# Attention queries turned once in the projection, and the row of maxima moved within SBUF

## The chip, the core and the metric

The kernel runs on one core of one Trainium2 chip. The metric is the device time of one execution in microseconds. Engines are called by the profile's names: PE (matmuls), DVE (vector work), ACT (activations and copies), POOL (vector work of the GpSimd engine), SP (it issues DMAs).

## What is computed

One layer of a transformer over 2048 latent tokens with 256 context tokens, width 1024, all in float32. A modulated RMSNorm feeds one projection whose columns are keys, values, queries, two halves of a gated MLP and two gates. Attention has eight query heads on two key/value heads, 64 wide; queries and keys are normalised and rotated (rope). A merge and a squared-ReLU MLP follow. What the change touches:

```python
q_x = apply_rope(rmsnorm(q_heads(q_x), q_norm_g[l]), cos, sin) * q_scale
k_all = jnp.concatenate([k_c, k_x], axis=2)
v_all = jnp.concatenate([v_c, v_x], axis=2)
attn_x = merge_heads(attend_blocked(q_x, k_all, v_all))   # softmax over 2304 keys
```

## The kernel before

A float32 operand is split into a high part (the cast to the fast matmul type) and a remainder, and products are sums of several matmuls. The span has three stretches: the projection with the gated MLP's mixing and the first part of the gates (to about 757 us), attention (to about 1436 us), and merge and MLP.

**In the projection**, `queries_work` (L770) treats one block of 512 tokens at a time, four blocks in all: it loads the raw queries, normalises them and applies rope on DVE in two halves c of 256 columns, tokens on the partitions. Each half is stored by SP to the DRAM tensor `q_d`, shaped [512 tokens, 512 columns] per block (L788). Such helpers are generators; the main loop of matmuls advances them step by step, and a scheduler then fixes the order on each engine by priority and dependences.

**Attention** runs over 16 units, one per block of 512 queries and pair of heads. A unit works through 18 tiles j of 128 keys in three groups of six (`GROUP`). Scores are made turned, with keys on the partitions and queries along the row, in two accumulating matmuls per head: `first` (L2034) multiplies the stacked high and low keys by `qa`, a tile in which the high part of a head's turned queries stands twice, in partitions 0 to 63 and 64 to 127; `second` (L2053) multiplies by `qb`, whose row 0 holds the negated maximum of each query, rows 1 to 63 zeros and rows 64 to 127 the turned remainder. The keys' counterpart of row 0 is a row of ones, from `lead`. So the maximum is subtracted inside the matmul, and ACT takes the exponential at once (L2057). `values` (L2067) follow after each group, sums of exponentials are added up on POOL and DVE (L2083, L2080).

What a unit needs is prepared by the units ahead of it. `load` brings a unit's queries from `q_d` in one transfer (L1948) and clears a tile `pb` on POOL (L1956). `cast` writes the high part twice into `pa` on ACT (L1959), and `remainder` writes the low part into `pb` on DVE (L1962). `queries` turns `pa` with eight transposes on PE (the helper at L189, `ident` is the identity) and two copies on ACT (L1974) into `qa`. `maxima` multiplies queries by keys a second time, unturned (L1999), and reduces on DVE (L2010, L2005 for the context). `reference` reduces these to one number per query (L2016) and writes it negated into column 0 of `pb` (L2017). `low_queries` turns `pb` with eight more transposes and two copies into `qb`.

`attend` (L1124) writes the order out by hand: in unit i, the unit after the next (`far`) is loaded in group 0 behind tile 2, its `cast` and `remainder` come in group 0, its `queries` in group 1 behind tile 8; the next unit's (`nxt`) `reference` ends group 1, its `low_queries` come in group 2 behind tile 17. PE and DVE keep the written order inside attention (`order`); the other engines are ordered by the scheduler. For units 0 and 1 the same steps are placed in `tail` (L1758), at the end of the projection. In units 1 to 4 DVE also works on the modulation weights (`mod`, L364, L368) in the middle of groups. The score banks of PSUM come from a rotating set of eight.

Of the kernel before, what the change touches and what calls it, by code (L numbers as in the profile page):

```python
# [10 lines left out]
F32 = mybir.dt.float32  # L11
F32R = mybir.dt.float32r
# [39 lines left out]
def f32(ap):  # L52
    return ap.bitcast(F32)
# [17 lines left out]
class Kern:  # L71
# [119 lines left out]
    def constants(self):  # L191
# [8 lines left out]
        nc.vector.memset(self.ones, 1.0)  # L200
        self.lead = cp.tile([P, 1], F32, name="lead")
        nc.vector.memset(self.lead, 0.0)
        nc.vector.memset(self.lead[0:1], 1.0)
        self.G1 = cp.tile([P, KC, 2], F32, name="G1")
        self.S1 = cp.tile([P, KC, 2], F32, name="S1")
        self.G2 = cp.tile([P, KC], F32, name="G2")
# [8 lines left out]
        def spill(n, shape):  # L215
            return [dp.tile(shape, F32, tag=f"{n}{b}", name=f"{n}_d{b}") for b in range(NB)]

        self.q_d = spill("q", [TB, NH * HD])
        self.gm_d = spill("gm", [512, TB])
        self.at_d = spill("at", [512, TB])  # L220
        self.ta_d = spill("ta", [D, TB])
# [548 lines left out]
    def queries_work(self, b):  # L770
        nc = self.nc
        q = [self.m4([TT, 4, HD]) for _ in range(2)]
        flat = [x.rearrange("p t h d -> p t (h d)") for x in q]
        src = self.pr_d[0][b]
        nc.sync.dma_start(flat[0][:, :, :P], self.rows(src[0], slice(2 * P, 3 * P)))
        nc.sync.dma_start(flat[0][:, :, P:], self.rows(src[1], slice(0, P)))
        nc.sync.dma_start(flat[1], self.rows(src[1], slice(P, 3 * P)))
        yield
        yield
        rbs = self.heads_rstd(q, 1.0 / HD)  # L780
        yield
        tabs = self.rope_tables("q", b)
        for c, (raw, rb) in enumerate(zip(q, rbs)):
            nc.vector.tensor_tensor(out=raw, in0=raw, in1=rb, op=ALU.mult)
            yield
            qo = self.m4([TT, 4, HD])
            self.rope(tabs, raw, qo, self.m4([TT, 4, HD]), 4)
            nc.sync.dma_start(  # L788
                self.rows(self.q_d[b], slice(c * 256, (c + 1) * 256)),
                qo.rearrange("p t h d -> p t (h d)"),  # L790
            )
            yield

    def raw_values(self, b, j, c):
        x = self.m4([TT, 4, HD])
# [328 lines left out]
    def attend(self, units, late, mod):  # L1124
        self.psum({"b": 8})
        begin = self.here()
        pend = []
        for i, u in enumerate(units):
            at = lambda n: units[n] if 0 <= n < len(units) else None
            nxt, far, old, older = at(i + 1), at(i + 2), at(i - 1), at(i - 2)  # L1130
            for gi, g in enumerate(range(0, NKT, GROUP)):
                group = range(g, g + GROUP)
                step = nxt if gi < 2 else far
                for j in group:
                    u.first(j)
                    u.second(j)
                    if j % GROUP == 2 and far:
                        if gi == 0:
                            far.load()
                        elif gi == 1:  # L1140
                            far.queries()
                    if not nxt:
                        next(late, None)
                    elif i and j % GROUP == 4:
                        next(mod, None)
                if gi == 2 and nxt:
                    nxt.low_queries()
                if step:
                    step.maxima(3)
                for f in pend:  # L1150
                    f()
                if gi == 0 and far:
                    far.cast()
                if gi == 2 and old:
                    old.sums()
                if step:
                    step.maxima(3)
                if gi == 0:
                    if older:
                        older.inverse()  # L1160
                    if far:
                        far.remainder()
                if gi == 1:
                    if nxt:
                        nxt.reference()
                    if old:
                        old.join()
                pend = [lambda u=u, j=j: u.values(j) for j in group]
            pend.append(u.leave)
        for _ in mod:  # L1170
            pass
# [558 lines left out]
    def build(self):  # L1730
# [27 lines left out]
        def tail(g, p):  # L1758
            u, v = units[0], units[1]
            n = KC - 2  # L1760
            if (g, p) == (n + 1, 0):
# [1 line left out]
                key_load(0)  # L1763
                u.cast()
                u.remainder()
            elif (g, p) == (n, 1):
                u.queries()
            elif (g, p) == (n + 1, 1):
                low_load(0)
            elif (g, p) == (n, 5):  # L1770
# [1 line left out]
            elif g >= n and p not in (0, 1):  # L1772
                if (g, p) == (n + 1, 5):
# [1 line left out]
                    v.cast()  # L1775
                    v.remainder()
                    value_load((0, 1))
                if (g, p) == (n, 6):
                    v.queries()
# [6 lines left out]
                if (g, p) == (n + 1, 3):  # L1786
                    u.maxima(len(u.todo))
                    u.reference()
                    u.low_queries()
                    v.maxima(6)  # L1790

        self.project(tail)
# [142 lines left out]
class Unit:  # L1935
# [8 lines left out]

    def load(self):
        k, nc = self.k, self.nc
        self.qt = k.t2([TT, 2, HD])
        nc.sync.dma_start(  # L1948
            self.qt.rearrange("p t h d -> p t (h d)"),
            k.q_d[self.b].rearrange("(t p) c -> p t c", p=P)[  # L1950
                :, :, self.p * P : (self.p + 1) * P
            ],
        )
        self.pa = k.t4([TT, 2, 2, HD], F32R)
        self.pb = k.t4([TT, 2, P])
        nc.gpsimd.memset(self.pb[:, :, :, :HD], 0.0)  # L1956

    def cast(self):
        self.nc.scalar.copy(self.pa, self.qt.unsqueeze(3).broadcast_to([P, TT, 2, 2, HD]))  # L1959

    def remainder(self):
        self.nc.vector.tensor_tensor(  # L1962
            out=self.pb[:, :, :, HD:], in0=self.qt, in1=f32(self.pa[:, :, :, 0, :]),
            op=ALU.subtract,
        )

    def turned(self, src):
        k = self.k
        out = []
        for h in range(2):  # L1970
            ps = k.bank([TB])
            k.transposes(ps, [src(t, h) for t in range(TT)])
            q = k.h2([TB], F32R)
            self.nc.scalar.copy(q, ps)  # L1974
            out.append(q)
        return out

    def queries(self):
        self.qa = self.turned(
            lambda t, h: f32(self.pa[:, t, h]).rearrange("p a d -> p (a d)")  # L1980
        )
        self.mx = self.k.small([TT, 2, NB + 1])

    def maxima(self, n):
        k, nc = self.k, self.nc
# [26 lines left out]
                    )  # L2012

    def reference(self):
        nm = self.k.small([TT, 2])
        self.nc.vector.tensor_reduce(out=nm, in_=self.mx, axis=AX.X, op=ALU.max)  # L2016
# [158 lines left out]
```

## Time and profile before

| | |
|---|---|
| time, median of 3 runs | 3094.04 us (3090.9 to 3099.88) |
| profiled execution, time | 3104.55 us |
| its span | 3102.5 us |
| its mean granted clock on PE | 0.983 |
| PE busy | 2994.0 us, 97% |
| DVE busy | 2074.6 us, 67% |
| ACT busy | 1459.5 us, 47% |
| POOL busy | 689.0 us, 22% |

Times in the profile are microseconds from the start of the span of one profiled execution. A row of the timeline gives start, duration, engine, line of the kernel, operation, what is written and read, shapes and count, and in brackets the idle time ahead of it with what ended it. Matmuls overlap, so the time that PE spends on one is read from the start of it to the start of the next.

### The profile page before, as it was taken

What the parts mean: (1) busy time and instruction counts of PE and PEld (TensorE: products, weight loads), DVE (VectorE), ACT (ScalarE), POOL (GpSimd) and SP (SyncE); (2) the same over time, 40 slices, a digit from 0 to 9 for tenths busy, and PEclk for the clock granted to TensorE, in tenths of its full rate; (3) what the DMA queues carried; (4) which work ended last, traced back from release to release, by engine and by line L of the source; (5) the groups of instructions that cost most, each with busy time, mean ns of one, the idle gap of its engine ahead of it and who ended that gap; (6) DMA issues with size and microseconds to landing.
All of it is one profiled execution on the core that took longest, in us unless ns stands there. A gap on an engine that the chain in (4) does not pass through costs nothing.

```text
span 3102.5 us, 38027 instructions
## 1 busy us (share of the span) xinstructions
PE 2994.0 (97%) x13501; PEld 2262.9 (73%) x13501; DVE 2074.6 (67%) x2990; ACT 1459.5 (47%) x2352; POOL 689.0 (22%) x506
## 2 busy tenths in 40 slices
PE   6999999979999999999989999999999999999999
PEld 4877788766555555556867878887878888878887
DVE  4767578875887667777654478775676666654555
ACT  5645765654555454554222155443454344444432
POOL 0000000001988888885134300000000000000000
PEclk9999999999999999999999999999999999999999
DMA  8676666644110000005865448887776544438554
GB/s 296 202 259 212 226 197 198 205 145 129 35 35 28 14 15 8 11 15 185 265 203 164 137 156 316 310 301 278 256 234 220 191 153 153 154 139 285 204 200 153
DMA packets 386478, 534.32 MB, mean 172 GB/s; under 512 B 32928, under 2 KB 204112, under 8 KB 386288
## 3 DMA queue, kind: packets, MB, share of 16 engines
q1 hardware_dynamic: 376512, 515.89, 49.7%
q10 hardware_dynamic: 9776, 16.01, 1.4%
q8 instruction: 106, 1.74, 0.2%
q14 instruction: 84, 0.69, 0.1%
HBM read 367.69 MB, written 164.10 MB: 171 GB/s over the span
## 4 chain that ended last, share of the span: by engine, by line
PE 83%; DMA 6%; DVE 5%; ACT 2%; issue 2%; POOL 1%; SPq 0%; ACTq 0%; DVEq 0%; POOLq 0%
PE b L1502 14%; PE b L1503 14%; PE b L1504 14%; PE b L2067 8%; PE b L2034 5%; PE b L2053 4%; PE b L183 3%; PE b L185 3%; PE b L184 3%; PE a L1502 3%; PE b L1999 3%; PE a L1503 3%; PE a L1504 3%; PE b L189 2%; DMA bw<-in_w_br_gm 1%
## 5 line engine op out<-in xcount | busy, mean ns | idle before, releaser
L2010 DVE TENSOR_REDUCE ts<-b 128x1 f32<-128x512 f32 x512 | 314.7, 681 | 141.6 <-PE b L1999 141.5
L2083 POOL TENSOR_TENSOR ac<-ac,p 128x512 f32<-128x512 f32 x216 | 301.5, 1428 | 67.7 <-ACT p L2057 67.0
L1608 DVE TENSOR_TENSOR b<-b,b 128x1024 fp32r<-128x1024 f32 x168 | 198.6, 1221 | 145.0 <-ACT b L1607 144.6
L1607 ACT CAST b<-b 128x1024 fp32r<-128x1024 f32 x168 | 168.7, 1051 | 240.0 <-PE b L1503 222.0
L2057 ACT ACTIVATE p<-b 128x512 f32<-128x512 f32 x384 | 199.8, 616 | 166.5 <-PE b L2053 156.6
L1502 PE MATMUL b<-b,b 128*128 128x512 f32 x672 | 263.9, 393 | 8.6 <-ACT b L1607 7.9
L1503 PE MATMUL b<-b,b 128*128 128x512 f32 x672 | 263.1, 391 | 2.4 <-DVE b L1608 2.4
L1504 PE MATMUL b<-b,b 128*128 128x512 f32 x672 | 262.6, 391 | 0.0
L2083 POOL TENSOR_TENSOR ac<-ac,t 128x512 f32<-128x512 f32 x152 | 217.6, 1457 | 0.0
L2034 PE MATMUL b<-h,h 128*128 128x512 f32 x576 | 200.9, 419 | 0.9 <-DVE ts L2010 0.4
L2053 PE MATMUL b<-h,h 128*128 128x512 f32 x576 | 180.3, 394 | 0.0
L2067 PE MATMUL b<-p,h 128*64 128x512 f32 x768 | 175.3, 598 | 0.0
L1503 PE MATMUL b<-hb,b 128*128 128x512 f32 x448 | 174.6, 390 | 0.0
L1956 POOL MEMSET t<- 128x512 f32 x16 | 8.4, 525 | 701.9 <-DMA tb_d<-t 679.8
L1502 PE MATMUL b<-hb,b 128*128 128x512 f32 x416 | 162.0, 389 | 0.0
L1504 PE MATMUL b<-hb,b 128*128 128x512 f32 x416 | 161.7, 389 | 0.0
L1512 DVE TENSOR_TENSOR f<-f,b 128x512 f32<-128x512 f32 x160 | 109.2, 682 | 77.7 <-issue 46.1
L1502 PEld LDWEIGHTS b<-b,b 128*128 128x128 f32 x672 | 126.9, 189 | 36.6 <-ACT b L1607 9.2
L2034 PEld LDWEIGHTS b<-h,h 128*128 128x128 f32 x576 | 106.7, 190 | 58.4 <-DVE ts L2010 19.4
L1503 PEld LDWEIGHTS b<-b,b 128*128 128x128 f32 x672 | 126.8, 189 | 30.0 <-DVE b L1608 3.7
L1504 PEld LDWEIGHTS b<-b,b 128*128 128x128 f32 x672 | 126.8, 189 | 26.5
L1502 PE MATMUL a<-f,h 128*128 128x384 f32 (+1 forms) x320 | 118.7, 376 | 12.8 <-ACT f L647 6.3
(409 smaller groups left out, 7435.0 us busy)
## 6 DMA issues: line engine op xcount, KB each, us to landing
ao_d<-f SPq DMA_DIRECT2D x224, 256.0 KB
f<-in_w_ff SPq DMA_DIRECT2D x48, 1024.0 KB
b<-ao_d SPq DMA_DIRECT2D x84, 512.0 KB
b<-w2o_d SPq DMA_DIRECT2D x84, 512.0 KB
w2o_d<-f SPq DMA_DIRECT2D x112, 256.0 KB
f<-in_w_in SPq DMA_DIRECT2D x44, 512.0 KB
f<-x_d SPq DMA_DIRECT2D x64, 256.0 KB
hb<-ao_d SPq DMA_DIRECT2D x56, 256.0 KB
```

The lines of the kernel that those rows point to most:

```text
L1502: mm(ps, wh, hh, start=start and k == 0, stop=False, skip_group_check=True)
L1503: mm(ps, wh, hl, start=False, stop=False, skip_group_check=True)
L1504: mm(ps, wl, hh, start=False, stop=k == len(w) - 1, skip_group_check=True)
L1512: nc.vector.tensor_tensor(out=out, in0=in0, in1=in1, op=op)
L1607: nc.scalar.copy(h, f32(l))
L1608: nc.vector.tensor_tensor(out=l, in0=f32(l), in1=f32(h), op=ALU.subtract)
L2010: nc.vector.tensor_reduce(out=self.mx[:, t, h, c : c + 1], in_=ps[h], axis=AX.X, op=ALU.max)
L2034: self.nc.tensor.matmul(self.pts[j][h], k.KA[c][self.kv][:, ks], self.qa[h], start=True, stop=False, skip_group_check=True,)
L2053: self.nc.tensor.matmul(s, k.KB[c][self.kv][:, ks], self.qb[h], start=False, stop=True, skip_group_check=True,)
L2057: self.nc.scalar.activation(pt[h], s, AF.Exp)
L2067: nc.tensor.matmul(self.o[h * HD : (h + 1) * HD, :], k.V[c][:, i, self.kv * HD : (self.kv + 1) * HD], pt[h], start=j == 0, stop=j == NKT - 1,)
L2083: nc.gpsimd.tensor_tensor(out=self.acc[e][:, h], in0=old[:, h], in1=pt[h], op=ALU.add)
```

## The change

In `queries_work` each rotated half is now turned on PE, four transposes for each pair of heads, copied from PSUM by ACT and stored through ACT's DMA queue, so that `q_d` holds, for each block and pair, the queries turned: 128 rows (two heads of 64) by 512 tokens. A unit's `load` fetches each head's 64 rows twice, into both halves of a tile's partitions, in four transfers on SP. `cast` (two copies on ACT, now in group 1) gives `qa` directly, `remainder` (two subtractions on DVE, now at the end of group 2) gives `qb` directly. `pa`, `pb` and `low_queries` go. The remainder also stands in rows 0 to 63 of `qb` now; rows 1 to 63 meet zeros of `lead`. Row 0 is overwritten with the maxima by the new `leading`, placed behind tile 14: one transpose of 128x8 to 8x128 on PE, a copy on ACT, and eight transfers of 512 bytes within SBUF on SP, each to a stretch of 128 queries in row 0. The sign of the maxima moves into `lead`, which is -1 instead of 1, so L2017 goes.

```diff
-        nc.vector.memset(self.lead[0:1], 1.0)
+        nc.vector.memset(self.lead[0:1], -1.0)
...
-        self.q_d = spill("q", [TB, NH * HD])
+        self.q_d = [
+            [dp.tile([P, TB], F32, tag=f"q{b}_{p}", name=f"q_d{b}_{p}") for p in range(NH // 2)]
+            for b in range(NB)
+        ]
...
             self.rope(tabs, raw, qo, self.m4([TT, 4, HD]), 4)
-            nc.sync.dma_start(
-                self.rows(self.q_d[b], slice(c * 256, (c + 1) * 256)),
-                qo.rearrange("p t h d -> p t (h d)"),
-            )
-            yield
+            yield
+            for f in range(2):
+                ps = self.bank([TB])
+                self.transposes(
+                    ps,
+                    [
+                        qo[:, t, 2 * f : 2 * f + 2].rearrange("p h d -> p (h d)")
+                        for t in range(TT)
+                    ],
+                )
+                ot = self.t2([TB])
+                nc.scalar.copy(ot, ps)
+                nc.scalar.dma_start(self.q_d[b][2 * c + f], ot)
...
-                    if j % GROUP == 2 and far:
-                        if gi == 0:
-                            far.load()
-                        elif gi == 1:
-                            far.queries()
+                    if j % GROUP == 2 and far and gi == 0:
+                        far.load()
+                    if j % GROUP == 2 and nxt and gi == 2:
+                        nxt.leading()
...
-                if gi == 2 and nxt:
-                    nxt.low_queries()
...
-                if gi == 0 and far:
+                if gi == 1 and far:
                     far.cast()
...
-                    if far:
-                        far.remainder()
+                if gi == 2 and far:
+                    far.remainder()
...
     def load(self):
         k, nc = self.k, self.nc
-        self.qt = k.t2([TT, 2, HD])
-        nc.sync.dma_start(
-            self.qt.rearrange("p t h d -> p t (h d)"),
-            k.q_d[self.b].rearrange("(t p) c -> p t c", p=P)[
-                :, :, self.p * P : (self.p + 1) * P
-            ],
-        )
-        self.pa = k.t4([TT, 2, 2, HD], F32R)
-        self.pb = k.t4([TT, 2, P])
-        nc.gpsimd.memset(self.pb[:, :, :, :HD], 0.0)
+        self.raw = [k.t2([TB]) for _ in range(2)]
+        for h, raw in enumerate(self.raw):
+            src = k.q_d[self.b][self.p][h * HD : (h + 1) * HD]
+            for i in range(2):
+                nc.sync.dma_start(raw[i * HD : (i + 1) * HD], src)
 
     def cast(self):
-        self.nc.scalar.copy(self.pa, self.qt.unsqueeze(3).broadcast_to([P, TT, 2, 2, HD]))
+        self.qa = [self.k.h2([TB], F32R) for _ in range(2)]
+        for q, raw in zip(self.qa, self.raw):
+            self.nc.scalar.copy(q, raw)
+        self.mx = self.k.small([TT, 2, NB + 1])
 
     def remainder(self):
-        self.nc.vector.tensor_tensor(
-            out=self.pb[:, :, :, HD:], in0=self.qt, in1=f32(self.pa[:, :, :, 0, :]),
-            op=ALU.subtract,
-        )
+        self.qb = [self.k.h2([TB], F32R) for _ in range(2)]
+        for q, hi, raw in zip(self.qb, self.qa, self.raw):
+            self.nc.vector.tensor_tensor(out=q, in0=raw, in1=f32(hi), op=ALU.subtract)
...
     def reference(self):
-        nm = self.k.small([TT, 2])
-        self.nc.vector.tensor_reduce(out=nm, in_=self.mx, axis=AX.X, op=ALU.max)
-        self.nc.vector.tensor_scalar(
-            out=self.pb[:, :, :, 0:1], in0=nm.unsqueeze(3), scalar1=-1.0, scalar2=None,
-            op0=ALU.mult,
-        )
-
-    def low_queries(self):
-        self.qb = self.turned(lambda t, h: self.pb[:, t, h, :])
+        k, nc = self.k, self.nc
+        self.nm = k.small([2, TT])
+        nc.vector.tensor_reduce(
+            out=self.nm.rearrange("p h t -> p t h"), in_=self.mx, axis=AX.X, op=ALU.max
+        )
+
+    def leading(self):
+        k, nc = self.k, self.nc
+        n = 2 * TT
+        ps = k.bank([P])
+        nc.tensor.transpose(ps[:n], self.nm.rearrange("p h t -> p (h t)"), k.ident)
+        row = k.t2([P])
+        nc.scalar.copy(row[:n], ps[:n])
+        for h in range(2):
+            for t in range(TT):
+                nc.sync.dma_start(
+                    f32(self.qb[h])[0:1, t * P : (t + 1) * P],
+                    row[h * TT + t : h * TT + t + 1],
+                )
```

In `tail` the calls of `queries` go, and `low_queries` becomes `leading`.

More of the change, by code (lines that the diff above doesn't have):

```diff
@@ L1765, in tail @@
                 u.remainder()
-            elif (g, p) == (n, 1):
-                u.queries()
             elif (g, p) == (n + 1, 1):
@@ L1777, in tail @@
                     value_load((0, 1))
-                if (g, p) == (n, 6):
-                    v.queries()
                 if (g, p) == (n + 1, 6):
@@ L1788, in tail @@
                     u.reference()
-                    u.low_queries()
+                    u.leading()
                     v.maxima(6)
@@ L1946, in load @@
         k, nc = self.k, self.nc
-        self.qt = k.t2([TT, 2, HD])
-        nc.sync.dma_start(
-            self.qt.rearrange("p t h d -> p t (h d)"),
-            k.q_d[self.b].rearrange("(t p) c -> p t c", p=P)[
-                :, :, self.p * P : (self.p + 1) * P
-            ],
-        )
-        self.pa = k.t4([TT, 2, 2, HD], F32R)
-        self.pb = k.t4([TT, 2, P])
-        nc.gpsimd.memset(self.pb[:, :, :, :HD], 0.0)
+        self.raw = [k.t2([TB]) for _ in range(2)]
[3 more added lines that the diff above has]
+                nc.sync.dma_start(raw[i * HD : (i + 1) * HD], src)
     def cast(self):
-        self.nc.scalar.copy(self.pa, self.qt.unsqueeze(3).broadcast_to([P, TT, 2, 2, HD]))
+        self.qa = [self.k.h2([TB], F32R) for _ in range(2)]
+        for q, raw in zip(self.qa, self.raw):
+            self.nc.scalar.copy(q, raw)
+        self.mx = self.k.small([TT, 2, NB + 1])
     def remainder(self):
-        self.nc.vector.tensor_tensor(
-            out=self.pb[:, :, :, HD:], in0=self.qt, in1=f32(self.pa[:, :, :, 0, :]),
-            op=ALU.subtract,
-        )
[L1967 to L1980, printed above, removed]
-        )
-        self.mx = self.k.small([TT, 2, NB + 1])
+        self.qb = [self.k.h2([TB], F32R) for _ in range(2)]
+        for q, hi, raw in zip(self.qb, self.qa, self.raw):
+            self.nc.vector.tensor_tensor(out=q, in0=raw, in1=f32(hi), op=ALU.subtract)
     def maxima(self, n):
```

## The prediction

> **What bounds the kernel now.** I read the page's first part, then the busy times by stretch (projection, attention, the rest), then the timeline of one steady unit of attention, PE, DVE and ACT in turn, and last the projection's waits.
>
> ```profile
> span 3102.5 us, 38027 instructions
> PE 2994.0 (97%) x13501; PEld 2262.9 (73%) x13501; DVE 2074.6 (67%) x2990; ACT 1459.5 (47%) x2352; POOL 689.0 (22%) x506
> ```
>
> ```profile
> 757.00:1436.00 679.00, 677.08 (x3184) 374.29 (x3184) 511.49 (x678) 354.86 (x687) 581.22 (x421) 0.99 0.08 25
> 0.00:757.00 757.00, 694.41 (x3238) 562.98 (x3239) 516.31 (x960) 423.94 (x688) 2.27 (x9) 0.97 0.65 212
> ```
>
> After a stretch's length come the busy times of PE, PEld, DVE, ACT and POOL. In attention PE is busy 677.08 of 679.00 us: what PE no longer does there comes off the time, unless what follows on PE waits for another engine. In the projection 62.6 us of PE are idle. I change nothing behind 1436 us.
>
> One steady unit on PE (start, duration, engine, line):
>
> ```profile
> 1098.98 0.88 PE L2034 MATMUL b<-h,h 128*128 128x512 f32 x2
> ...
> 1112.58 0.73 PE L2034 MATMUL b<-h,h 128*128 128x512 f32 x2
> ...
> 1115.44 1.03 PE L189 MATMUL b<-ident,t 128*128 128x128 f32 x8
> 1116.23 0.71 PE L2034 MATMUL b<-h,h 128*128 128x512 f32 x2
> ...
> 1120.17 3.65 PE L2067 MATMUL b<-p,h 128*64 128x512 f32 x16
> ...
> 1126.37 0.88 PE L2034 MATMUL b<-h,h 128*128 128x512 f32 x2
> ...
> 1129.67 0.63 PE L2034 MATMUL b<-h,h 128*128 128x512 f32 x2
> ...
> 1132.40 1.04 PE L189 MATMUL b<-ident,t 128*128 128x128 f32 x8
> 1133.37 1.39 PE L1999 MATMUL b<-h,h 64*128 64x256 f32 x10
> 1134.69 3.65 PE L2067 MATMUL b<-p,h 128*64 128x512 f32 x16
> ...
> 1141.74 0.89 PE L2034 MATMUL b<-h,h 128*128 128x512 f32 x2
> 1142.46 0.63 PE L2053 MATMUL b<-h,h 128*128 128x512 f32 x2
> ```
>
> The unit runs from 1098.98 to 1141.74, 42.76 us, its groups beginning at 1098.98, 1112.58 and 1126.37. Two sets of eight transposes stand in it: the queries (1115.44 to 1116.23, 0.79 us) and the low queries (1132.40 to 1133.37, 0.97 us).
>
> **The transposes that go.** All sixteen leave the unit: 0.79 + 0.97 = 1.76 us, over 16 units 28.2 us, the most that attention can give. What is late next decides how much arrives. In the second group nothing is queued between the transposes and the values at 1120.17 but matmuls and exps, and the two evictions on ACT go with the transposes. I take all of it, 0.8 us.
>
> ```profile
> 1126.01 3.68 DVE L2010 TENSOR_REDUCE ts<-b 128x1 f32<-128x512 f32 x6 [1.36 <-PE b L1999]
> 1129.72 0.20 DVE L2016 TENSOR_REDUCE ts<-ts 128x8 f32<-128x40 f32 x1
> ...
> 1127.58 4.19 ACT L2057 ACTIVATE p<-b 128x512 f32<-128x512 f32 x8 [6.98 <-PE b L2053]
> 1131.63 2.10 ACT L2057 ACTIVATE t<-b 128x512 f32<-128x512 f32 x4
> 1133.53 1.16 ACT L1974 CAST h<-b 128x512 fp32r<-128x512 f32 x2
> ```
>
> In the third group 0.97 us go, but a wait is added: the single transpose of the maxima stands behind tile 14 on PE, at 1129.67 by the old times, and wants L2016's result, ready at 1129.92. So PE stalls about 0.25 to 0.4 us (PE's group begins earlier by as much as the reduces do), then works about 0.1 us (0.97 / 8 = 0.12). Queued behind it on PE are tiles 15 to 17 and all that follows. The values behind them cannot start much before their exps and banks: ACT's twelve exps end at 1133.73, and one row copy more is put among them. That leaves a gain of 0.97 − 0.4 − 0.1 = 0.5 us. Taking all, 14 steady second groups and 15 third groups, and 2.5 us for the sets that stand ahead of the attention (two units' queries, one unit's low queries, 0.79 to 0.97 each): 11.2 + 7.5 + 2.5 = **−21.2 us**, bounds −28.2 and −12 (if the third group gives nothing).
>
> **Casts and subtractions.** ACT loses a cast of 128x1024 and four evictions per unit and gets two casts and a short copy; it is busy 354.86 of 679 us, so this is worth nothing. POOL loses a memset. DVE loses L2017 and gets one subtraction more, and both move to the end of the third group:
>
> ```profile
> L1962 DVE TENSOR_TENSOR t<-t,t x16: 692/1640/1668, 702.9 to 1330.4; 128x512 f32<-128x512 f32 x16
> ```
>
> ```profile
> 1141.38 3.68 DVE L2010 TENSOR_REDUCE ts<-b 128x1 f32<-128x512 f32 x6 [2.20 <-PE b L1999]
> 1148.38 1.89 DVE L2010 TENSOR_REDUCE ts<-b 128x1 f32<-128x512 f32 x3 [3.32 <-PE b L1999]
> ...
> 930.58 3.40 DVE L368 SCALAR_TENSOR_TENSOR raw<-raw,silu,raw 128x512 f32<-128x512 f32 x2
> 934.03 3.68 DVE L2010 TENSOR_REDUCE ts<-b 128x1 f32<-128x512 f32 x6
> ```
>
> The source view gives minimum, median and maximum: 0.69 us while POOL was still idle, 1.64 us beside POOL's adds. The Trainium skill says the same of the pair (GPSIMD Engine Reference, "1. Specifications": GpSimd shares its SBUF interfaces with VectorE, with contention where DVE has two SBUF inputs), and the trace agrees with its 0.69 and 1.64. Two subtractions are 3.28 us; the hole they move into is the idle of 3.32 us ahead of 1148.38. That fits, with nothing to spare. In units 1 to 4 the hole is taken: L368's 3.40 us stand there (930.58), with reduces directly behind that must free banks for PE. DVE's 3.28 us push these; gaps like the 2.20 us ahead of 1141.38 take up the greater part, and I take 1 us for each of four units, **+4 us** (0 to +10).
>
> **Eight row transfers.** They are no PE work, but the next unit's L2053 wants the row. The copy on ACT follows tile 14's exps, six of the eight in the 4.19 us from 1127.58, so about 1130.7, 4.4 us into the group. The next unit's first L2053 (1142.46) is 16.1 us into it, 15.6 after the gain. That leaves 11.2 us for eight issues and a landing.
>
> ```profile
> L1948 SPq DMA_DIRECT2D t<-q_d x16: 359/426/498, 690.5 to 1242.8; - x16
> ```
>
> ```profile
> 666.95 0.92 SPq L796 DMA_DIRECT2D m<-p_d x2
> ...
> 670.48 0.63 ACT L807 ACTIVATE t<-m 128x512 f32<-128x512 f32 x1 [0.91 <-DMA m<-p_d]
> ```
>
> An issue on SP takes 0.36 to 0.50 us, eight at most 4.0; the two loads issued from 666.95 were used at 670.48, at most 3.5 us. So 7.5 of 11.2 us: covered, 0. If the cover were gone each microsecond over it would cost 15 us. Four loads instead of one per unit add three issues on SP. What SP holds ahead of the row transfers in its written order (loads of w_mod in units 1 to 4, loads of queries) waits for steps that lie before the maxima, so they are not held up. Not so for the first unit:
>
> ```profile
> 738.50 11.83 SPq L1879 DMA_DIRECT2D tb_d<-m  x4
> ...
> 757.78 1.05 PE L2053 MATMUL b<-h,h 128*128 128x512 f32 x2
> ```
>
> Its row stands on SP behind the projection's last stores, issued until 750.33; 7.5 us from there is 757.8, and the first L2053, at 757.78, should come about 2 us earlier: **+2 us** (0 to +6).
>
> **The projection.** It gets 64 transposes and 16 copies and stores on ACT, and loses eight stores on SP. The stores left SP waiting for the rope; their issues now stand on ACT, behind their own copies.
>
> ```profile
> 199.16 1.22 DVE L498 TENSOR_TENSOR m<-m,m 128x1024 f32<-128x1024 f32 x1
> ...
> 203.77 1.22 DVE L498 TENSOR_TENSOR m<-m,m 128x1024 f32<-128x1024 f32 x1
> ...
> 218.34 1.36 PE L189 MATMUL b<-ident,m 128*128 128x128 f32 x8 [2.60 <-DVE m L754]
> 219.35 0.78 PE L1503 MATMUL a<-f,h 128*128 128x512 f32 x1
> ...
> 418.90 0.69 PE L1502 MATMUL a<-f,h 128*128 128x384 f32 x1 [3.02 <-ACT a L662]
> ...
> 576.14 1.22 DVE L498 TENSOR_TENSOR m<-m,m 128x1024 f32<-128x1024 f32 x1
> ...
> 678.18 0.80 PE L1502 MATMUL a<-hx,e 128*128 128x512 f32 x1 [5.43 <-DVE t L1920]
> ```
>
> Eight transposes take 0.79 us (above) to 1.01 us (218.34 to 219.35): 64 take 6.3 to 8.1. PE's written order puts block 0's sixteen at about 199.5 in the old time, and its ropes end at 200.4 and 205.0: a wait of up to 4.5 us. By the same comparison it is 1 to 2 us in block 1, almost none in block 2, and in block 3 (rope done at 577.4, place about 574) 3 to 6. Together 15 to 20 us are put into PE's row. Against that, PE waits already stand behind each place and are ended by other engines (2.60, 3.02 and 5.43 us in the rows above): what delays PE ahead of them is swallowed there as far as the releaser does not itself hang on PE. The gaps after blocks 0 and 1 should swallow all of theirs; of the 5 to 8 us of blocks 2 and 3, the wait of 5.43 swallows part. I take **+3 us**, bounds −6 (SP freed earlier) and +10.
>
> **The sum.** −21.2 + 4 + 2 + 3 = −12.2 us. The profiled execution took 3104.55 us, 10.5 above the median of the runs (3094.04): profile 3092, median **3081.8**.
>
> **Rivals.** *The transposes are worth their row means.*
>
> ```profile
> L189 PE MATMUL b<-ident,t x296: 270/272/329, 22.8 to 1388.7; 128*128 128x128 f32 x148
> ```
>
> By that a transpose is 0.272 us; 256 go and 64 come, −192 × 0.272 = −52 us, 3042. The Trainium skill has about this price (TensorE: Matmul & The Clock Gate, "Part 4: PE-mode transpose": about 275 ns in a kernel's context). Against it: eight in 0.79 us, so the records overlap and each holds PE about 0.1 us. Chance 0.05.
>
> *The projection gives it back.* If the waits for the rope are not swallowed (+15 instead of +3) and the units with L368 cost 2 us: −21.2 + 8 + 2 + 15 = +3.8, 3098. For it: DVE is 68% busy in the projection and PE can do nothing that is written behind a transpose while that waits. Chance 0.20.
>
> *The row comes late: slower.* The eight small transfers are served one after another. It decides from 11.2 us on, 1.4 us each.
>
> ```profile
> 205.47 1.61 SPq L645 DMA_DIRECT2D f<-t_d  x1
> ```
>
> SP has an issue of 1.61 us; with it 8 × 1.61 + 3.5 = 16.4 us, 5.2 too late in 15 units, +78 − 12.2 = +66, 3160; the wait would stand before L2053. Against it: SP's issues in attention take 0.5 us at most, and that row stands where the DMA engines are loaded. The Trainium skill warns of such transfers (DMA: Bandwidth & Descriptors, "Rules for kernel authors": under 64 KB mostly overhead) and gives one about 2 us of fixed cost; by an estimate from that figure, eight in series would be 16 us, 4.8 late, 72 us in all, and eight overlapped are covered. No run here shows which. Chance 0.13, with a lesser lateness that gives back only the gain inside it.
>
> *It moves nothing on the path*: the values in each group are held by exps and banks, so PE's shorter queue waits where the transposes stood. Then the other terms' +9 stays: 3103. Against it: PE has no wait of size in the groups. Chance 0.07.
>
> **How the numbers follow.** Forecast 0.55, rivals 0.05, 0.20, 0.13, 0.07. A measurement of this kernel tells about 0.3%, 9.3 us, from no change. The forecast's own range is 3062 (all 28.2 and −4 from the projection) to 3092; a tenth of it ends within 0.3%. Faster: 0.55 less 0.04, 0.05, and 0.02 of the projection's case, 0.58. Slower: 0.12 of the late row, 0.03 of the projection's case, 0.04 of the last, 0.19. The rest, 0.23, is the same. The range leaves out the first rival and most of the late row: 3060 to 3104.
>
> **What would show it.** Right: L189 on t falls from 296 to about 40, the unit's period from 42.76 to about 41.3 us, a PE wait of 0.3 to 0.4 us at the new transpose, none at L2053, the two subtractions at 1.64 us in DVE's old hole. Wrong: L2053 waiting for a DMA; gaps on PE at the queries' transposes in the projection, and 678 us not where it was; PE waiting on DVE's reduces behind the subtractions in the units before 950 us; a period that stays.

## The result and the profile after

| | before | after |
|---|---|---|
| time, median (first comparison, 8 runs each) | 3095.86 us (3090.9 to 3099.88) | 3087.22 us (3082.92 to 3090.86) |
| ratio, 95% interval | | 0.9974 (0.9963 to 0.9985) |
| second comparison, another chip (26 and 12 runs) | 3098.95 us | 3091.88 us, 0.998 (0.9966 to 0.9994) |
| profiled execution | 3104.55 us | 3086.31 us |

The change makes the kernel 8.6 us or 0.26% faster, clear of zero by its interval and just under the 0.3% that the prediction named as the bound; the forecast was 12.2 us. The two first profiles differ by 18.2 us, twice that, because the profile of before was one of its longest executions. A second profile of each, and those of the experiments, help to tell chance from effect.

The page's first lines of after, and its busy times by stretch (length, then PE, PEld, DVE, ACT, POOL, with counts):

```profile
span 3084.1 us, 37934 instructions
...
PE 2969.0 (96%) x13325; PEld 2234.8 (72%) x13325; DVE 2094.8 (68%) x2990; ACT 1443.3 (47%) x2336; POOL 690.1 (22%) x490
```

```profile
0.00:755.40 755.40, 697.28 (x3278) 566.25 (x3278) 518.96 (x961) 430.92 (x701) 0.70 (x6) 0.97 0.65 211
755.40:1423.70 668.30, 654.10 (x2968) 347.44 (x2968) 531.73 (x678) 332.24 (x660) 584.74 (x408) 0.99 0.10 32
```

The second stretch is cut at the first scores and at the first matmul of the merge. Of its 668.30 us PE is idle in 14.2, where it was idle in 1.9 of 679 us before: half of that stands in one wait at its end, shown below.

The same unit on PE as in the prediction (L2028 and L2047 are the two score matmuls, L2009 the transpose of the maxima, L2061 the values):

```profile
1089.37 0.89 PE L2028 MATMUL b<-h,h 128*128 128x512 f32 x2
...
1102.99 0.73 PE L2028 MATMUL b<-h,h 128*128 128x512 f32 x2
...
1109.59 3.65 PE L2061 MATMUL b<-p,h 128*64 128x512 f32 x16
...
1115.79 0.89 PE L2028 MATMUL b<-h,h 128*128 128x512 f32 x2
...
1118.63 0.62 PE L2047 MATMUL b<-h,h 128*128 128x512 f32 x2
1119.48 0.27 PE L2009 MATMUL b<-ident,ts 128*8 128x128 f32 x1 [0.23 <-DVE ts L2001]
1119.51 0.71 PE L2028 MATMUL b<-h,h 128*128 128x512 f32 x2
...
1123.52 3.65 PE L2061 MATMUL b<-p,h 128*64 128x512 f32 x16
...
1130.57 0.89 PE L2028 MATMUL b<-h,h 128*128 128x512 f32 x2
1131.30 0.63 PE L2047 MATMUL b<-h,h 128*128 128x512 f32 x2
```

The groups start at 1089.37, 1102.99 and 1115.79, the next unit at 1130.57: 13.62, 12.80 and 14.78 us, where they were 13.60, 13.79 and 15.37. The unit went from 42.76 to 41.20 us. The transpose has its wait for the reduce; from the end of tile 14 (two matmuls of 0.23 us behind 1118.63, so 1119.09) to 1119.51 it costs 0.42 us.

PE's end of attention and the start of the merge, and SP's first loads of branch weights, after and then before:

```profile
1414.40 1.89 PE L2061 MATMUL b<-h,h 128*64 128x512 f32 x8
1423.67 0.79 PE L183 MATMUL b<-in,bw 128*128 128x512 f32 x1 [7.38 <-ACT bw L150]
...
1419.06 0.39 SPq L1224 DMA_DIRECT2D bw<-in_w_br_attn  x1
```

```profile
1411.23 0.58 SPq L1216 DMA_DIRECT2D bw<-in_w_br_attn  x1
...
1436.74 0.50 PE L183 MATMUL b<-in,bw 128*128 128x512 f32 x1 [1.75 <-ACT bw L150]
```

Before, SP issued these loads 25.5 us ahead of their use, after only 4.6. PE waits 7.38 us instead of 1.75. Why SP was late stands in its waits:

```profile
SPq L1224 <- DMA at_d<-t: 26.5, 1, 26.5
```

It waited 26.5 us for the store of the last unit's output. The first weight buffer of the merge lies over slots of attention's set `t2`. The change allots more tiles from this set, five in each unit instead of three, and so the last unit's output tile came to lie in the slot under that buffer.

All profiles by stage, read off PE's starts: the first score, from there to the last unit's first score, from there to the merge.

| kernel | first score | to last unit | to merge |
|---|---|---|---|
| before, two profiles | 756.8, 751.6 | 638.3, 638.5 | 41.7, 41.7 |
| after, two profiles | 755.4, 762.6 | 620.6, 619.7 | 47.7, 47.6 |
| late transpose (tile 15) | 759.6 | 615.0 | 49.1 |
| slot moved | 758.4 | 620.3 | 42.1 |
| subtractions parted | 756.9 | 624.5 | 42.1 |
| subtractions later | 754.5 | 621.5 | 43.4 |
| three edits | 754.3 | 616.9 | 43.8 |
| four edits | 759.1 | 612.0 | 43.6 |
| chain laid open | 753.9 | 714.2 | 52.1 |
| projection's part alone, in before | 769.3 | 639.0 | 41.7 |
| without the turning | 756.3 | 619.2 | 42.1 |
| turning two steps later | 785.7 | 619.9 | 42.1 |

The attention columns repeat within 1 us where a kernel was profiled twice. The first column, at the end of 750 us of projection, varies by several us between kernels whose projection is the same.

For the projection there is a finer mark: the main loop's matmuls come in a fixed number, so the one with the same number can be sought in each profile (the three lines of `product`, L1502 to L1504 in before, counted in PE's order). The last column is the time from number 2500 to number 2620, 655.8 to 707.7 us in the first profile of before.

| kernel | behind before (mean of its two) at 2500 | at 2620 | from 2500 to 2620 |
|---|---|---|---|
| before, two profiles | | | 51.9, 51.9 |
| nine with after's projection (after's two, seven experiments) | 10.9 on average (7.3 to 15.8) | 4.6 (1.3 to 10.0) | 44.5 to 46.4 |
| projection's part alone, in before | 15.4 | 14.0 | 50.5 |
| without the turning | 3.1 | 3.1 | 51.9 |

### The profile page after: what moved, and what is told of

Read it like the earlier page. It is cut to its first block, busy times and chain, and to the rows that moved or that the text cites. A ratio compares the mean times of both kernels' runs of the same rounds, so it can differ in the third digit from the quotient of the medians.

```text
span 3084.1 us, 37934 instructions
## 1 busy us (share of the span) xinstructions
PE 2969.0 (96%) x13325; PEld 2234.8 (72%) x13325; DVE 2094.8 (68%) x2990; ACT 1443.3 (47%) x2336; POOL 690.1 (22%) x490
## 5 line engine op out<-in xcount | busy, mean ns | idle before, releaser
L2077 POOL TENSOR_TENSOR ac<-p,p 128x512 f32<-128x512 f32 x32 | 47.4, 1502 | 773.7 <-ACT p L2051 773.5
L2028 PE MATMUL b<-h,h 128*128 128x512 f32 x576 | 202.5, 421 | 3.4 <-DVE ts L1994 2.1
L2047 PE MATMUL b<-h,h 128*128 128x512 f32 x576 | 180.0, 394 | 0.0
L2061 PE MATMUL b<-p,h 128*64 128x512 f32 x768 | 175.3, 598 | 0.0
L2028 PEld LDWEIGHTS b<-h,h 128*128 128x128 f32 x576 | 106.6, 190 | 62.4 <-DVE ts L1994 25.9
```

The lines of the kernel that those rows point to most:

```text
L2028: self.nc.tensor.matmul(self.pts[j][h], k.KA[c][self.kv][:, ks], self.qa[h], start=True, stop=False, skip_group_check=True,)
L2047: self.nc.tensor.matmul(s, k.KB[c][self.kv][:, ks], self.qb[h], start=False, stop=True, skip_group_check=True,)
L2061: nc.tensor.matmul(self.o[h * HD : (h + 1) * HD, :], k.V[c][:, i, self.kv * HD : (self.kv + 1) * HD], pt[h], start=j == 0, stop=j == NKT - 1,)
L2077: nc.gpsimd.tensor_tensor(out=self.acc[e][:, h], in0=old[:, h], in1=pt[h], op=ALU.add)
```

## The experiments

All ratios are to before on the same chip: one chip for the first four kernels, then one for each four that follow.

**The projection's part alone.** Added to before's `queries_work`, behind its store:

```diff
+            for f in range(2):
+                ps = self.bank([TB])
+                self.transposes(ps, [qo[:, t, 2 * f : 2 * f + 2]... for t in range(TT)])
+                ot = self.t2([TB])
+                nc.scalar.copy(ot, ps)
+                nc.scalar.dma_start(self.qt_d[b][2 * c + f], ot)
```

> The kernel before, with the projection's part of the change added: each rotated half is also turned on PE (64 transposes, 16 copies and 16 stores on ACT's queue, to DRAM that nobody reads; the eight old stores stay, attention is the old one). Theory (the wait for mixing work at 665 to 697 us swallows what PE loses in the projection): PE runs 7 to 10 us late at about 660 us and 0 to 2 us late at the start of attention; time 0 to 3 us above before. Rival (the projection gives it away, and attention hides it): the start of attention comes 7 to 10 us late, time 7 to 10 us above before.

3115.39 us against 3099.02, ratio 1.0056 (1.0043 to 1.007): slower by 16.4 us, and the first score at 769.3. The theory falls in this kernel: PE is 15.4 us behind at main-loop matmul 2500, and only 1.4 of them are given back by 2620. The 16.4 us are more than the rival gave, too. In the kernels with after's projection 5.5 to 7.4 us are given back in the same stretch. This kernel keeps the eight old stores on SP, which after has not; that they make the difference is not shown. So its 16 us are not the price of turning in after.

**The slot.**

```diff
-        oc = k.t2([TB])
+        oc = (k.h2 if self.last else k.t2)([TB])
```

> The kernel after, with one tile moved: the last unit's output tile is taken from the large set of slots of the keys instead of the small set that the branch weights' first buffer overlaps after attention. Theory (that overlap, with the store of this tile, holds SP's first load of branch weights until 1419 us, and PE waits 7.4 us where before it waited 1.8): the load is issued 6 to 10 us before attention's last matmul and PE's wait falls to about 2 us, time 5 to 6 us under after. Rival (the merge waits for its loads anyhow): PE's wait moves to the next loads, time as after, within 2 us.

3083.93 us, 0.9956 (0.9943 to 0.997), against 0.9974 for after: 5.6 us better by the two ratios, which come from two comparisons. The trace shows the cause apart from their noise:

```profile
1395.22 0.58 SPq L1224 DMA_DIRECT2D bw<-in_w_br_attn  x1
...
1420.79 0.50 PE L183 MATMUL b<-in,bw 128*128 128x512 f32 x1 [1.81 <-ACT bw L150]
```

The load goes out 25.6 us ahead of the merge and the wait is 1.81 us, that of before. The stretch to the merge is 42.1 us instead of 47.7. The theory holds.

**The transpose one tile later.**

```diff
-                    if j % GROUP == 2 and nxt and gi == 2:
+                    if j % GROUP == 3 and nxt and gi == 2:
```

> The kernel after, with the transpose of the maxima one tile later on PE (behind tile 15 instead of 14). Theory (PE stalls 0.39 us in each unit for the reduce that ends at that moment): the third group falls from 14.78 to about 14.4 us, 15 units, 5 to 6 us under after, and no wait at the second score matmul, since the row still lands some 3 us early. Rival (the group's end is set by the exps on ACT and their banks): the group stays within 0.1 us of 14.78 and the time at that of after.

```profile
1120.33 0.61 PE L2047 MATMUL b<-h,h 128*128 128x512 f32 x2
1120.79 0.27 PE L2009 MATMUL b<-ident,ts 128*8 128x128 f32 x1
1120.81 0.70 PE L2028 MATMUL b<-h,h 128*128 128x512 f32 x2
```

The stall is gone: the transpose follows at once and holds PE for 0.02 us. The third group takes 14.46 us, 0.32 less, and attention up to the last unit 615.0 us instead of 620.6. Of these 5.6 us the start of the merge takes back 1.4 (49.1 instead of 47.7). The time, 3088.38 us or 0.9967 (0.9956 to 0.9978), is 2.2 us better than after by ratio, with intervals as wide as the gain; the stage shows it, the time alone would not.

**The subtractions parted**, one to the end of group 1 and one to the middle of group 2:

```diff
                 if gi == 1:
                     ...
+                    if far:
+                        far.remainder((0,))
...
+                if gi == 2 and far:
+                    far.remainder((1,))
                 if gi == 2 and old:
                     old.sums()
```

> The kernel after, with the two subtractions parted: one at the end of group 1 behind the maxima's reduce, one in the middle of group 2, instead of both at the end of group 2. Theory (in units 1 to 4 they push the modulation's steps and the reduces behind them): units 1 to 4 fall from 42.10 to 43.14 us to 41.2 to 42.2, 4 to 5 us in all, the other units stay at 41.2. By the build's slots the first load of branch weights is also free of the last unit's store here, so PE's wait ahead of the merge should be about 2 us too, 5 to 6 us more: together 9 to 11 under after. Rival (DVE is simply full in these units, wherever the subtractions stand): units 1 to 4 stay.

3091.9 us, 0.9983 (0.9974 to 0.9992): no better than after (0.9974), though the start of the merge is free (42.1). Units 1 and 3 went from 42.1 to 41.5 us, as the theory has it, but units 2 and 4 to 46.8 and 45.6. There the second subtraction delays the reduces across the unit's border:

```profile
926.05 1.74 DVE L1969 TENSOR_TENSOR h<-t,h 128x512 fp32r<-128x512 f32 x1
927.72 2.47 DVE L1999 TENSOR_REDUCE ts<-b 128x1 f32<-128x512 f32 x4
```

```profile
928.45 0.80 PE L2033 MATMUL b<-h,h 128*128 128x512 f32 x1 [2.47 <-DVE ts L1999]
```

PE waits 2.47 us for a bank that a reduce holds. In these units DVE's order decides, but it is not enough to find a hole in a unit without the modulation's steps.

**The subtractions later**, at the end of the next unit's group 0:

```diff
-                if gi == 2 and far:
-                    far.remainder()
...
+                    if nxt and i:
+                        nxt.remainder()
```

> The kernel after, with the two subtractions a third of a unit later: at the end of the next unit's group 0, where the single one stood before the change. Theory (where they stand decides; that place has an idle of 2.2 us behind the old subtraction of 1.64 us, and lies behind the modulation's steps): units 1 to 4 fall from 42.10 to 43.14 us to 41.2 to 41.9, 3 to 4 us in all; the other units stay at 41.2. By the build's slots the branch weights are free of the last unit's store here too, 5 to 6 us more: 8 to 10 under after. Rival (DVE is full in these units): they stay, 5 to 6 under after from the slots alone.

3085.68 us, 0.9954 (0.9942 to 0.9966). Units 2 and 4 fell from 43.1 to 41.95 us, units 1 and 3 rose from 42.1 to 44.5 and 44.3: there modulation steps follow in group 1 and the reduces come late again. The gain over after is no more than that of the slot, which is free here too (43.4 to the merge), though this edit moves no such tile. Neither theory nor rival had units 1 and 3 right.

**Three edits together** (this place of the subtractions, the transpose behind tile 15, the slot):

> Three edits together: the subtractions at the end of the next unit's group 0, the maxima's transpose behind tile 15, the last unit's output tile in the large set of slots. Theory (the three costs lie in different places and add up): attention 8 to 9 us shorter than in after, the merge begins 5 to 6 us sooner behind it, 13 to 15 us under after, a ratio to before of 0.993. Rival (what is saved goes into the merge's loads, as after's saving partly did): 6 to 9 under after.

3086.09 us, 0.9958 (0.9946 to 0.9971): no better than the slot alone by its time, and short of the 13 to 15 us that the theory gave. The stages did add up (616.9 and 43.8), but units 1 and 3 take 44.5 and 44.3 us. One of these stalls shows a second price:

```profile
821.52 0.50 PE L2028 MATMUL b<-h,h 128*128 128x512 f32 x1 [1.24 <-DVE ts L1994]
```

```profile
821.00:826.00 5.00, 4.48 (x12) 3.28 (x13) 4.96 (x8) 2.42 (x5) 5.00 (x5) 0.67 0.00 0
823.00:826.00 3.00, 3.00 (x8) 2.32 (x9) 2.96 (x5) 1.78 (x4) 3.00 (x4) 0.50 0.00 0
826.00:830.00 4.00, 4.00 (x24) 2.88 (x22) 3.96 (x3) 3.96 (x9) 4.00 (x3) 0.99 0.01 2
```

In the column behind the engines stands the granted clock: 0.67 over the 5 us around and behind the stall's end, 0.50 in the last three of them, 0.99 behind that.

**Without the turning.**

```diff
-                ps = self.bank([TB])
-                self.transposes(ps, [...])
-                ot = self.t2([TB])
-                nc.scalar.copy(ot, ps)
-                nc.scalar.dma_start(self.q_d[b][2 * c + f], ot)
+                nc.sync.dma_start(
+                    self.q_d[b][2 * c + f].rearrange("p (t c) -> p t c", t=TT),
+                    qo[:, :, 2 * f : 2 * f + 2].rearrange("p t h d -> p t (h d)"),
+                )
```

> The kernel after without the projection's turning: the rotated halves are stored by SP, unturned, into the place of the turned ones (16 stores of 256 KB, no transposes, copies or ACT stores), so the queries that attention reads are not the right ones. Theory (PE loses 9 to 13 us in the projection by 660 us, and the mixing work behind it gives most of it back): PE is level with before at 660 us, and attention starts 0 to 3 us sooner than in after's kernels (755.4 to 759.6 us). By the build's slots the branch weights are free here, so the time is to be held against the slot experiment: 0 to 3 us under it. Rival (what PE loses in the projection is lost): 8 to 12 us under it.

3074.88 us, 0.9927 (0.9915 to 0.9939), 9 us under the slot experiment by ratio, with the two intervals some 3 to 15. That speaks for the rival. The profile speaks more for the theory: from matmul 2500 to 2620 this kernel takes 51.9 us, as before does, where the nine that turn take 44.5 to 46.4, so those do get back a part of their loss. Its first score stands at 756.3 us, within their spread, but at 195 us, ahead of any turning, it was already 3.5 us behind the first profile of before, where after was 0.8 behind. Counted from there, main-loop matmul 2700 (at 737 us) comes 5.5 us earlier than in the nine on average.

**The chain laid open**, the transpose at the end of group 2:

```diff
-                    if j % GROUP == 2 and nxt and gi == 2:
-                        nxt.leading()
...
+                if gi == 2 and nxt:
+                    nxt.leading()
                 if gi == 2 and far:
                     far.remainder()
```

> The kernel after, with the maxima's transpose at the very end of group 2, ahead of the next unit's first scores, so that the row's copy, eight transfers and landing lie open. Theory (issue 5.2 us for the eight, landing about 2 us, so the chain is about 8 us and in after ends some 3 us ahead of its use): PE waits 7 to 9 us at each unit's first second-score matmul, for DMA, 15 units, 95 to 130 us over after. Rival (the landing is long, 5 us or more, and after is close to the edge): 10 to 13 us each, 150 to 190 over after.

One execution, 3185.78 us, some 99 over after, at the low end of the theory; units take 47.9 to 49.2 us instead of 41.2.

```profile
1084.64 0.27 PE L2009 MATMUL b<-ident,ts 128*8 128x128 f32 x1
...
1085.35 4.95 SPq L2014 DMA_DIRECT2D h<-t  x8
...
1089.00 0.77 PE L2047 MATMUL b<-h,h 128*128 128x512 f32 x1 [2.88 <-DMA h<-t]
1091.41 0.79 PE L2047 MATMUL b<-h,h 128*128 128x512 f32 x1 [1.64 <-DMA h<-t]
```

The eight are issued from 1085.35 to 1090.30, 0.62 us each; the second head's matmul starts 1.1 us after the last issue. So the landing is about 1.1 us, and in after, where SP issues the eight by 1125.55, the row is there at 1126.7 for a use at 1131.30: 4.6 us to spare.

**The turning two steps later**, two more `yield` between rope and transposes:

> The kernel after, with the turning put two steps later behind the rope in the projection's helper, so that block 0's second set of transposes stands 32 matmuls behind the first instead of 8. By the build's slots the branch weights are free of the last unit's store here too, 5 to 6 us, so the time is to be held against the slot experiment. Theory (PE waits 4.4 us for rope in block 0, and 2.3 us for the copies queued behind; the mixing work gives about 5 us of the projection's loss back whatever its cause): PE at 225 us is 1 to 3 us behind before instead of 5, at 750 us as in after's kernels, time within 3 us of the slot experiment. Rival (what PE loses in the projection is lost): 4 to 7 us under the slot experiment.

3108.66 us, 1.0036 (1.0023 to 1.005): 25 us worse than the slot experiment, which neither theory nor rival had. PE did lose less: by the main-loop matmul at 226 us it was 1.6 us behind the first profile of before, where after was 8.7 behind, and by the one at 656 us 1.8 ahead. But PE then stood waiting:

```profile
698.47 0.55 PE L183 MATMUL b<-m,m 128*128 128x256 f32 x1 [18.26 <-DMA m<-ws_d]
...
724.11 0.55 PE L183 MATMUL b<-m,m 128*128 128x256 f32 x1 [21.05 <-DMA m<-ws_d]
```

The gated MLP's mixing comes behind the queries in the same chain of steps. Four more steps in each of four blocks pushed its last two chunks past the matmuls that had covered them.

**Four edits together**: the transpose behind tile 15, the last output tile and one sums' row in the larger set of slots (`h2`), and the later subtractions for units 2 and 4 alone:

```diff
-                    if j % GROUP == 2 and nxt and gi == 2:
+                    if j % GROUP == 3 and nxt and gi == 2:
...
+                    if nxt and i in (2, 4):
+                        nxt.remainder()
-                if gi == 2 and far:
+                if gi == 2 and far and i not in (1, 3):
...
-        oc = k.t2([TB])
+        oc = (k.h2 if self.last else k.t2)([TB])
...
-            row = k.t2([TB])
+            end = (self.b, self.p) == (NB - 1, NH // 2 - 2)
+            row = (k.h2 if end else k.t2)([TB])
```

> The kernel after with four edits: the maxima's transpose behind tile 15; the last unit's output tile and the last sums' row but one in the large set of slots; and the subtractions at the end of the next unit's group 0 in units 2 and 4 alone, elsewhere at the end of group 2. Theory (each cost lies in its own unit): units 1 and 3 at 41.8, units 2 and 4 at 41.6, the others at 40.88; PE's wait ahead of the merge about 2 us; together 13 to 15 us under after. Rival (the subtractions cost as much in units 1 and 3 again, as when they were moved in all units): units 1 and 3 at 43 or more, 9 to 11 under after.

3081.88 us, 0.9948 (0.9933 to 0.9963), and 10 us under after on the same chip (3091.88). Units 1 to 4 take 41.8, 41.5, 41.8 and 41.5 us, the others 40.87; the last unit's first score comes 612.0 us after the first, against 620 in after. The units are those of the theory. The saving of 8 us there and 4 us ahead of the merge is close to what the medians show, and less than the theory's 13 to 15 us. It beats both kernels, before and after; against the slot experiment (0.9956) its time is not told apart.

**Both kernels once more.**

> The kernel after, unedited, on the chip of the other three, so that they are held against it and not only against before. Theory (attention gives 18 us, the start of the merge takes 6 back, the projection 2 to 5): 8 to 10 us under before. Rival (the gap of 18 us between the two first profiles is the true one): 16 to 19 under.

> The kernel before, unedited: a second profile of it, since the first was one of its longest executions (3104.55 us). Theory (the first profile holds 3 to 9 us of chance in the projection and the stages behind attention): attention's units as in the first profile within 0.1 us, its start 2 to 5 us earlier than 756.8. Rival (the projection of before always takes this long, and the turning is free): start of attention within 1 us of 756.8.

After took 3091.88 us, 0.998 (0.9966 to 0.9994), 7 us under before: the theory, a little below its range. Before took 3098.87 us, 1.0002 (0.9992 to 1.0013), and its first score stands at 751.6 instead of 756.8, with the same attention. So the theory holds: the first profile of before held some 5 us of chance in the projection, and 3 more between merge and end (its last 1666 us are 1663 here). This second profile is not the median either: its time, 3096.65 us, is 2 us below that of its runs.

## Why the prediction was right, and where not

- **Transposes** (−0.8 and −0.5 us per unit): measured −0.99 and −0.59. The mechanism and the new wait were right (0.42 us of stall and transpose, forecast 0.35 to 0.5). Most of the further 0.2 us in the second group lies beside the transposes: the pair of score matmuls right behind them held PE for 0.54 us and the pair at its place now 0.45, the maxima's six matmuls 1.02 and now 0.94; why is not shown. The rival of 272 ns per transpose is refuted: 256 of them gone took 17.7 us and not 70 off the attention stretch. So is the rival by which the values hold each group: a steady unit is 1.6 us shorter. The bound of −12 for this term does not follow from its own numbers: without the third groups 21.2 − 7.5 = 13.7 are left.
- **Subtractions** (+4 us in units 1 to 4): these units exceed the steady one by 0.96, 1.95, 0.91 and 1.94 us; before by 0.00, 0.62, −0.01 and 0.63. That is +4.5 us. Right, and the experiments that moved the subtractions show that it is their place among the modulation's steps that costs. The subtraction still takes 1.69 us beside POOL:

```profile
L1966 DVE TENSOR_TENSOR h<-t,h x32: 680/1694/1777, 706.6 to 1341.6; 128x512 fp32r<-128x512 f32 x32
```

- **The row** (covered, 7.5 of 11.2 us): no score matmul waits for it. The issue was underrated and the landing overrated: 0.62 us each and 1.1 us, together 6.1, against 4.0 and 3.5. The 2 us that the prediction put on the first unit's row did not come: in the profile of after SP has issued its eight by 754.87, and the first L2047 starts at 756.45 without a wait, 0.5 us later than a landing of 1.1 us would allow. The rival of the late row was wrong by its premise, eight in series at 1.61 us.
- **The projection** (+3 us, with the steps ahead of attention +2.5): the first score stands at 757.2 us on average over nine profiles with this projection (after's two, seven experiments; 753.9 to 762.6) and at 754.2 over two of before: +3.0, from spreads of 5 to 9 us. The waits in block 0 are as foreseen, 0.74 and 3.61 us, together 4.35 where up to 4.5 were forecast; the next one was not foreseen:

```profile
201.46 1.09 PE L189 MATMUL b<-ident,m 128*128 128x128 f32 x8 [0.74 <-DVE m L501]
...
206.16 1.94 PE L189 MATMUL b<-ident,m 128*128 128x128 f32 x8 [3.61 <-DVE m L501]
...
210.43 0.79 PE L1510 MATMUL a<-f,h 128*128 128x512 f32 x1 [2.33 <-ACT a L665]
```

```profile
210.00:214.00 4.00, 3.57 (x9) 2.85 (x10) 1.41 (x5) 4.00 (x9) 0.00 (x0) 0.52 0.97 316
```

  Behind them ACT's copies are late by 2.33 us, and the granted clock is 0.52 for 4 us. The step that swallows the loss is half right. The gaps behind blocks 0 and 1 were to swallow all of theirs, and did not: the nine profiles are 10.3 us behind before at the main-loop matmul at 226 us and still 10.9 at 656 us. What comes back does so behind that, 6.3 us on average up to 708 us. In the first profile of each kernel it is 7.4 us: PE's waits there are 2.47, 1.24, 5.07 and 0.47 us where before had 1.25, 5.43, 1.60 and 5.60, which makes 4.6 us. A part of the rest is the granted clock behind the waits, before and then after in the 5 us in which the longer of the first two ends (0.50 and 1.00, the third number from the right):

```profile
678.00:683.00 5.00, 4.82 (x11) 3.80 (x12) 4.93 (x15) 2.62 (x3) 0.53 (x1) 0.50 0.14 52
```

```profile
678.00:683.00 5.00, 3.01 (x12) 2.18 (x12) 4.42 (x14) 0.77 (x2) 0.00 (x0) 1.00 0.09 32
```

  How much the turning costs by itself stays open between 3 us (by the first scores, with the other terms ahead of attention in it), 5.5 us (by the profile without it) and 9 us (by its time).
- **What was missing**: the start of the merge. "I change nothing behind 1436 us" looked at instructions and not at the slots that the added tiles turn. It cost 47.7 − 41.7 = +6.0 us, and the slot experiment gives 5.6 of it back.
- **The sum**: attention up to the last unit −17.7 (forecast −18.7 + 4 = −14.7), ahead of it +3.0 (+2.5), start of the merge +6.0 (0): −8.7, measured −8.6 and, on the other chip, −7.1. That it closes to 0.1 us is chance: the part ahead of attention is uncertain by several us, and the stretch behind the start of the merge, 1660.5 and 1661.3 us in after against 1665.8 and 1662.7 in before, stands in no term and varies from 1659 to 1672 over all kernels. The forecast of −12.2 was near it because a gain of 3 us that was too small and a loss of 6 that was missing partly cancelled.

## What to carry to other kernels

Read a stage's gain as the distance between repeated marks (here unit to unit, where most steady units agree to 0.05 us), and look at once at the first wait of the stage that follows: what was hidden behind the longer stage comes out there. An added tile in a rotating set changes which buffer lies over which, also for work far behind; the waits of the first loads after a change of pools show it, and one tile moved elsewhere mended it here. Steps that are added to a chain of helpers delay what follows in the chain, whatever they cost themselves.

## What the runs showed of the hardware

- A short stall can cost PE more than its length: behind waits of 3.61 and 2.33 us the granted clock was 0.52 for the next 4 us, and behind one of 1.24 us 0.67 for 5 us, before it was full again. It does not each time: behind the waits of 2.18 and 2.47 us that end at 648.90 and 678.83 in the profile of after it stayed at 1.00.
- The time of an issue on SP does not follow the bytes. In the profile of after the median is 0.59 us for 512 bytes within SBUF (first row) and 0.59 us for 128 KB from DRAM (second row); the 256 KB of before took 0.36 to 0.50 us. The small transfer is usable about 1.1 us after the end of its issue, as the laid-open chain shows.

```profile
L2014 SPq DMA_DIRECT2D h<-t x128: 497/587/1269, 749.9 to 1372.5; - x128
L1955 SPq DMA_DIRECT2D t<-q_d x64: 450/594/618, 692.4 to 1292.6; - x64
```

- PE holds a transpose of 128x8 for 0.02 us when its operand is ready, though its record lasts 0.27 us.
